# Gate and up products by seven block products instead of eight, with four feed-forward groups

## The chip, the cores and the metric

The kernel runs on one core of a Trainium2 chip. The metric is the device time of one execution in microseconds (us). Four engines matter here: TensorE (PE, with its weight loads shown as PEld), VectorE (DVE), ScalarE (ACT) and SyncE (SP), which only issues transfers. Each engine takes its instructions in the order in which the program lists them.

## The reference

One step of a two-layer network on 640 tokens (128 context tokens and 512 latent ones), in float32. Each layer is a feed-forward block, a mixer (an SSD scan with pooling in layer 0, a gated MLP with a convolution in layer 1) and a second feed-forward block. All three are modulated by vectors that come from `c` and `w_mod`. What the change touches is the feed-forward block, computed four times:

```python
def swiglu(h, w_gate, w_up, w_down):
    return (jax.nn.silu(h @ w_gate) * (h @ w_up)) @ w_down
# h (640, 1024), w_gate and w_up (1024, 2816), w_down (2816, 1024)
# x = x + 0.5 * gate * swiglu(modulate(rms_norm(x, g), shift, scale), ...)
```

## The kernel before

Activations lie transposed: eight tiles of 128 channels by 640 tokens hold the residual `x`. The tokens are worked on in two halves of 320, called A and B. Every float32 product is made of three TensorE products: each operand is split into a high part (a cast) and a low part (a subtraction), and `mm3` (L311 to L313) adds high by high, high by low and low by high into one PSUM bank. So a weight tile of 128 input rows by 128 output columns takes three matmuls of 320 columns for each half.

A feed-forward block (`ffn`) has 22 slices j of 128 hidden channels. For each slice, `run_units` makes gate and up for half A and then for half B, over eight input tiles k: 2 halves x 2 matrices x 8 x 3 = 96 matmuls. `post` then takes silu of gate on ScalarE (L551), multiplies by up on VectorE (L552) and splits the result with `split` (cast L296 on ScalarE, subtraction L297 on VectorE). The slices come in groups, `GROUPS`. After each group `out_phase` multiplies the group's slices by `w_down` for eight output tiles m and two halves, and `x_update` (L341) adds to `x`. The last group's out phase runs into `boundary`, which makes the next stage's modulated input: VectorE L303 and L307, ScalarE L305, first for half A and, while TensorE already works on A's first four weight units, for half B. The first four units are then used for half B too.

TensorE's order is the order of the program. VectorE, ScalarE and SyncE are ordered by Tile's scheduler before the run: an instruction whose inputs and buffers are there goes, and of several the one that is earlier in the program.

A weight unit is 128 x 1024 floats (512 KB). `load_raw` (L182) transfers it into a raw buffer, `load_unit` casts (L202) and subtracts (L203). A raw buffer is free again after its split. `W(key)` starts the loads of a unit and of the two after it in `plan`. The split tiles of gate and up units take two of the nine buffers of tag "w" each, and are free when TensorE has used them.

The modulation vectors are made on VectorE, next to all this: an item (`mod_item`) is a transfer of 512 KB (L247) into a buffer of the same raw tag and two multiply-and-reduce instructions (L250). There are 128 items. `pump(n)` emits the next n; `need_mod` emits until a given vector is done. In the first feed-forward block three are pumped per slice, later two, so all 128 are done within the third block. `odd`, the mixer of layer 1, begins with `boundary` and then `pump(1000)`, which finds none left; `even`, the mixer of layer 0, begins with `boundary` and `need_mod(0, 8)`, which finds that vector done.

## Time and profile before

| | us |
|---|---|
| median of 2 runs | 2660.35 (2659.68 to 2661.01) |
| span of the profiled execution | 2658.8 |
| TensorE busy | 2615.8 (98%) |
| VectorE busy | 1633.9 (61%) |
| ScalarE busy | 883.1 (33%) |
| transfers, mean over the span | 107 GB/s |

Read the busy shares first, then the chain of work that ended last, then busy time by stage. The stages follow each other at about 503 (first block ends, `even` begins), 853, 1315 (third block begins), 1784 (`odd` begins) and 2170 us. A busy time of TensorE counts pipelined matmuls that overlap, so the number of matmuls in a stretch says more than their durations.

### The profile page before, as it was taken

Reading aid. Unit: us, or ns where it says so; the run is one execution under the profiler, and the core shown is the slowest. Engines: PE = TensorE matmul, PEld = TensorE weight load, DVE = VectorE, ACT = ScalarE, POOL = GpSimd, SP = SyncE. Lnnn points to the kernel's source line nnn. Section 1 sums busy time; section 2 is a strip of 40 time slices with the busy share of each in tenths; the row PEclk is TensorE's granted clock in tenths of the full one; section 3 lists DMA queues with packets and bytes.
Section 4 is the critical chain, followed back from the end, with each engine's and each line's share of the span. In section 5 each row is a group of like instructions: output and inputs, shape, how many; then the busy total and the mean of one; then the engine's idle time right before and its main releaser. Section 6 shows DMA issues by size and latency. Waiting matters only on the chain.

```text
span 2658.8 us, 43502 instructions
## 1 busy us (share of the span) xinstructions
PE 2615.8 (98%) x18141; PEld 2550.1 (96%) x18141; DVE 1633.9 (61%) x2961; ACT 883.1 (33%) x1630; POOL 5.2 (0%) x83
## 2 busy tenths in 40 slices
PE   7999999999999999999999999999999999999998
PEld 5999999999989999999999999999879999999998
DVE  6866667698997755556675554265984764323325
ACT  4322222468854321212432121242222543212222
POOL 0000000000000000000000000000000000000000
PEclk9999999999999999999999999999999999999999
DMA  6553445111223333434243342224441132212211
GB/s 247 194 158 124 156 138 178 60 56 57 72 68 104 131 123 117 130 118 139 76 141 122 112 135 95 68 92 121 117 113 56 64 104 65 88 63 72 78 62 68
DMA packets 88228, 284.72 MB, mean 107 GB/s; under 512 B 11744, under 2 KB 18400, under 8 KB 87520
## 3 DMA queue, kind: packets, MB, share of 16 engines
q1 hardware_dynamic: 85072, 276.39, 32.3%
q10 hardware_dynamic: 2960, 5.56, 0.7%
q8 instruction: 142, 2.33, 0.4%
q14 instruction: 54, 0.44, 0.1%
HBM read 267.31 MB, written 3.67 MB: 102 GB/s over the span
## 4 chain that ended last, share of the span: by engine, by line
PE 95%; DVE 3%; ACT 1%; DMA 1%; issue 0%; ACTq 0%; DVEq 0%
PE ps L311 29%; PE ps L312 29%; PE ps L313 29%; PE ps L1075 1%; PE ps L502 1%; PE ps L962 1%; PE ps L1138 1%; PE ps L1140 1%; PE ps L1139 1%; PE ps L902 0%; PE ps L929 0%; PE ps L431 0%; DVE slab L307 0%; DVE tmp L303 0%; DVE tmp L291 0%
## 5 line engine op out<-in xcount | busy, mean ns | idle before, releaser
L312 PE MATMUL ps<-slab,wh 128*128 128x320 f32 (+1 forms) x5376 | 1662.1, 309 | 0.7 <-DVE slab L297 0.4
L311 PE MATMUL ps<-slab,wh 128*128 128x320 f32 x5280 | 1639.6, 311 | 1.1 <-DVE slab L966 0.9
L313 PE MATMUL ps<-slab,wl 128*128 128x320 f32 x5280 | 1632.2, 309 | 0.0
L312 PEld LDWEIGHTS ps<-slab,wh 128*128 128x128 f32 (+1 forms) x5376 | 1008.9, 188 | 3.6 <-DVE slab L297 0.9
L311 PEld LDWEIGHTS ps<-slab,wh 128*128 128x128 f32 x5280 | 990.9, 188 | 9.6 <-issue 4.5
L313 PEld LDWEIGHTS ps<-slab,wl 128*128 128x128 f32 x5280 | 990.6, 188 | 0.5
L203 DVE TENSOR_TENSOR wl<-wr,wh 128x1024 fp32r<-128x1024 f32 (+3 forms) x401 | 429.6, 1082 | 296.9 <-ACT wh L202 141.4
L202 ACT CAST wh<-wr 128x1024 fp32r<-128x1024 f32 (+3 forms) x401 | 369.1, 935 | 548.4 <-DMA wr<-in_wg 162.7
L250 DVE CUSTOM_DVE_ANT_0 junk<-wm,crow,cv 128x1024 bf16<-128x1024 f32 x256 | 328.4, 1283 | 127.3 <-DMA wm<-in_wm 123.6
L341 DVE SCALAR_TENSOR_TENSOR slab<-ps,mod,slab 128x128 f32<-128x128 f32 (+2 forms) x384 | 156.2, 434 | 217.2 <-PE ps L313 216.8
L296 ACT CAST slab<-tmp 128x320 fp32r<-128x320 f32 x200 | 90.6, 459 | 431.2 <-DVE tmp L552 424.4
L552 DVE TENSOR_TENSOR tmp<-tmp,ps 128x320 f32<-128x320 f32 x176 | 84.8, 484 | 204.9 <-PE ps L313 203.0
L551 ACT ACTIVATE tmp<-ps 128x320 f32<-128x320 f32 x176 | 76.2, 436 | 342.9 <-PE ps L313 342.7
L297 DVE TENSOR_TENSOR slab<-tmp,slab 128x320 fp32r<-128x320 f32 x200 | 96.8, 490 | 65.9 <-ACT slab L296 65.6
L1082 DVE SCALAR_TENSOR_TENSOR cacc<-pad,cv,cacc 128x655 f32<-128x655 f32 x112 | 100.9, 901 | 4.2 <-ACT cacc L1078 0.7
L280 ACT ACTIVATE tmp<-slab 128x320 f32<-128x320 f32 x112 | 53.2, 475 | 145.3 <-DVE slab L341 133.3
L284 DVE TENSOR_TENSOR tmp<-tmp,tmp 128x320 f32<-128x320 f32 x98 | 47.9, 490 | 37.4 <-ACT tmp L280 37.4
L305 ACT ACTIVATE slab<-tmp,mod 128x128 fp32r<-128x128 f32 (+1 forms) x120 | 50.4, 468 | 45.1 <-DVE tmp L303 43.8
L307 DVE SCALAR_TENSOR_TENSOR slab<-tmp,mod,slab 128x128 fp32r<-128x128 f32 (+1 forms) x120 | 46.6, 432 | 0.7 <-ACT slab L305 0.7
L303 DVE SCALAR_TENSOR_TENSOR tmp<-slab,mod,tmp 128x128 f32<-128x128 f32 (+1 forms) x120 | 46.8, 435 | 0.1
L647 DVE SCALAR_TENSOR_TENSOR cacc<-pad,cv,cacc 128x642 f32<-128x642 f32 x48 | 42.3, 882 | 1.5 <-ACT cacc L641 1.1
L311 PE MATMUL ps<-ydh,wh 128*128 128x320 f32 x128 | 39.7, 310 | 0.0
(201 smaller groups left out, 1229.1 us busy)
## 6 DMA issues: line engine op xcount, KB each, us to landing
wm<-in_wm SPq DMA_DIRECT2D x128, 512.0 KB, 3.8
wr<-in_wg SPq DMA_DIRECT2D x88, 512.0 KB, 4.0
wr<-in_wu SPq DMA_DIRECT2D x88, 512.0 KB, 3.5
wr<-in_wd SPq DMA_DIRECT2D x64, 448.0 KB, 3.3
wr<-in_wd SPq DMA_DIRECT2D x32, 512.0 KB, 4.1
wr<-in_wei SPq DMA_DIRECT2D x24, 512.0 KB, 3.5
wr<-in_woi SPq DMA_DIRECT2D x24, 512.0 KB, 4.1
rep<-pad SPq DMA_DIRECT2D x128, 83.4 KB, 2.8
```

The costliest lines, as they stand in the source:

```text
L202: S.copy(hi, raw[:, k0:k1, :])
L203: V.tensor_sub(lo, raw[:, k0:k1, :], hi)
L250: V.tensor_tensor_reduce(out=junk, in0=w, in1=mst["crow"][cond], scale=1.0, scalar=cvc("b_mod", L * 72 + idx * KC + c), op0=ALU.mult, op1= ...
L296: S.copy(hi, src)
L297: V.tensor_sub(lo, src, hi)
L311: TE.matmul(ps, lhsT=wh, rhs=xh, start=start, stop=False)
L312: TE.matmul(ps, lhsT=wh, rhs=xl, start=False, stop=False)
L313: TE.matmul(ps, lhsT=wl, rhs=xh, start=False, stop=stop)
L341: V.scalar_tensor_tensor(out=x[m][:, a:b], in0=ps[:, a - o:b - o], scalar=mcol(L, gidx, m, cond), in1=x[m][:, a:b], op0=ALU.mult, op1=ALU.add)
L551: S.activation(out=sg, in_=pg[:, :TH], func=AF.Silu)
L552: V.tensor_mul(sg, sg, pu[:, :TH])
L1082: V.scalar_tensor_tensor(out=ac, in0=pad[:, i:i + 655], scalar=cvc("dw_w", i * 8 + j), in1=ac, op0=ALU.mult, op1=ALU.add)
```

## The change

Gate and up of one slice are seen as a product of 2 x 2 blocks: the input channels in two halves (k 0 to 3, k 4 to 7), the tokens in halves A and B, the columns in gate and up. The eight block products (k half x token half x matrix) become seven, P1 to P7, by the Strassen-Winograd scheme, for slices j >= 2 of every block. The sums of weight blocks (`load_sums`) and of input blocks (`full` and the lines after it) are made on chip and split again. Products accumulate in three PSUM banks per slice; ScalarE copies intermediate results out (`tap`), VectorE combines them. `product_order` interleaves two slices. A sum unit takes two raw buffers and six "w" buffers. `w_down` units now take "w" buffers as well, and raw buffers are three for the whole program. Modulation items are pumped one per slice in the first block only, and one per output tile m in every out phase but a block's last. The pool of the modulation tiles moves from the right side of memory to the left, under the stage's own pool. There are four groups instead of three. The other edits rename slabs as pairs or quads of the same data.

```diff
-GROUPS = ((0, 8), (8, 15), (15, 22))
+GROUPS = ((0, 6), (6, 12), (12, 17), (17, 22))
...
+                        if j < NSTD:
+                            add_unit(("g", L, f, j), ap["wg"][L, f, j], 8, 128)
+                            add_unit(("u", L, f, j), ap["wu"][L, f, j], 8, 128)
+                        else:
+                            add_unit(("s", L, f, j), (ap["wg"][L, f, j], ap["wu"][L, f, j]), 8, 128)
...
+            raw = wpool.tile([P, n, m], F32, tag="raw", name=nm("wr"), bufs=RB)
...
+        def load_sums(key):
+            src, n, m = units[key]
+            g, u = raw_tile(src[0], n, m), raw_tile(src[1], n, m)
+            ph = state["pool"]
+            x1 = w_split(g, 8, m, tag="w", bufs=WB)
+            s31 = ph.tile([P, 8, m], F32, tag="s31", name=nm("ws"), bufs=1)
+            s24 = ph.tile([P, 8, m], F32, tag="s24", name=nm("ws"), bufs=1)
+            V.tensor_add(s31[:, 4:8, :], u[:, 0:4, :], u[:, 4:8, :])
+            V.tensor_add(s31[:, 0:4, :], u[:, 0:4, :], g[:, 0:4, :])
+            x2 = w_split(s31, 8, m, tag="w", bufs=WB)
+            V.tensor_add(s24[:, 0:4, :], g[:, 0:4, :], s31[:, 4:8, :])
+            V.tensor_add(s24[:, 4:8, :], g[:, 4:8, :], s24[:, 0:4, :])
+            x3 = w_split(s24, 8, m, tag="w", bufs=WB)
+            x4 = w_split(u[:, 4:8, :], 4, m, tag="w2", bufs=4, pool=ph)
+
+            def half(x, i):
+                return x[0][4 * i:4 * i + 4], x[1][4 * i:4 * i + 4]
+            loaded[key] = dict(P1=half(x1, 0), P2=half(x1, 1), P7=half(x2, 0), P5=half(x2, 1),
+                               P6=half(x3, 0), P3=half(x3, 1), P4=x4)
...
         def W(key):
-            prefetch(index[key] + LOOK)
+            i, left = index[key], LOOK
+            prefetch(i)
+            while i + 1 < len(plan) and left > 0:
+                i += 1
+                left -= 2 if plan[i][0] == "s" else 1
+                if wpos[0] <= i and plan[i][0] == "s" and not state.get("sums"):
+                    break
+                prefetch(i)
             return loaded[key]
...
-            w = state["raw"].tile([P, D], F32, tag="raw", name=nm("wm"), bufs=state["rb"])
+            w = wpool.tile([P, D], F32, tag="raw", name=nm("wm"), bufs=RB)
...
-        def out_phase(keys, sh, sl, L, gidx, last, nxt=None, lag=3):
+        def out_phase(keys, sh, sl, L, gidx, last, nxt=None, lag=3, items_per=0):
             if not last:
                 for m in range(8):
                     for H in (A, B):
                         out_task(H, m, keys[m], sh, sl, L, gidx, False)
+                    pump(items_per)
                 return None
...
+        CHAIN = (("P1", "P6", "P7", "P4"), ("P5", "P3"), ("P2",))
+
+        def product_order(js):
+
+            at = {j: [0, 0, 0] for j in js}
+            since = {}
+            out = []
+            while any(at[j][c] < len(CHAIN[c]) for j in js for c in range(3)):
+                t = len(out)
+                live = [j for j in js if any(at[j][c] < len(CHAIN[c]) for c in range(3))][:2]
+                cand = [(j, c) for j in live for c in range(3) if at[j][c] < len(CHAIN[c])]
+                cand = [(j, c) for j, c in cand if c == 0 or at[j][0] > 0]
+                ready = [jc for jc in cand if t - since.get(jc, -9) >= 3]
+                j, c = ready[0] if ready else min(cand, key=lambda jc: since.get(jc, -9))
+                out.append((j, CHAIN[c][at[j][c]]))
+                since[j, c] = t
+                at[j][c] += 1
+            return out
...
+            f12, f22, f11 = full(0, B), full(1, B), full(0, A)
+            V.tensor_sub(f22, f22, f12)
+            V.tensor_sub(f12, f11, f12)
+            V.scalar_tensor_tensor(out=f11, in0=f22, scalar=-1.0, in1=f11, op0=ALU.mult, op1=ALU.subtract)
+            X = dict(P1=hn.t[0, A], P2=hn.t[1, A], P3=hn.t[1, B])
+            X["P5"] = t_split(f12, ph, "T", 6)
+            X["P6"] = t_split(f11, ph, "T", 6)
+            X["P7"] = t_split(f22, ph, "T", 6)
+            f21 = full(1, A)
+            V.scalar_tensor_tensor(out=f21, in0=f11, scalar=-1.0, in1=f21, op0=ALU.mult, op1=ALU.subtract)
+            X["P4"] = t_split(f21, spool, "s", None)
...
+                for j, p in product_order(js):
+                    if p == "P1":
+                        W(("s", L, f, j))
+                    wh, wl = loaded["s", L, f, j][p]
+                    xh, xl = X[p]
+                    b = "a" if p in CHAIN[0] else "c" if p in CHAIN[1] else "b"
+                    if (j, b) not in bank:
+                        bank[j, b] = psum()
+                    ps = bank[j, b]
+                    first = p in ("P1", "P5", "P2")
+                    final = p in ("P4", "P3", "P2")
+                    for k in range(4):
+                        for n, (l, r) in enumerate(((wh, xh), (wh, xl), (wl, xh))):
+                            TE.matmul(ps[:, :TH], lhsT=l[k], rhs=r[:, k, :], start=(first and k == 0 and n == 0),
+                                      stop=(k == 3 and n == 2), skip_group_check=True)
+                    with tc.high_priority(offset=TAP_EARLY):
+                        if p in ("P1", "P6", "P7", "P5"):
+                            got[j, p] = tap(ps)
+                        if p == "P2":
+                            V.tensor_add(got[j, "P1"], ps[:, :TH], got[j, "P1"])
+                            S.activation(out=got[j, "P1"], in_=got[j, "P1"], func=AF.Silu)
+                        if p == "P3":
+                            V.tensor_add(got[j, "P6"], ps[:, :TH], got[j, "P6"])
+                            S.activation(out=got[j, "P6"], in_=got[j, "P6"], func=AF.Silu)
+                        if (p == "P7" and (j, "P5") in got) or (p == "P5" and (j, "P7") in got):
+                            V.tensor_add(got[j, "P7"], got[j, "P7"], got[j, "P5"])
+                        if p == "P4":
+                            hf = ph.tile([P, T], F32, tag="hf", name=nm("hf"), bufs=1)
+                            V.scalar_tensor_tensor(out=hf[:, SL[A]], in0=ps[:, :TH], scalar=-1.0, in1=got[j, "P1"],
+                                                   op0=ALU.mult, op1=ALU.mult)
+                            V.scalar_tensor_tensor(out=hf[:, SL[B]], in0=got[j, "P7"], scalar=-1.0,
+                                                   in1=got[j, "P6"], op0=ALU.mult, op1=ALU.mult)
+                            h_tile(j)
+                            split(hf, hts[j][:, 0, :], hts[j][:, 1, :])
+                    if p == "P1" and (L, f) == (0, 0):
+                        pump(1)
...
             for gi, (j0, j1) in enumerate(GROUPS):
-                for j in range(max(j0, 2), j1):
-                    for H in (A, B):
-                        pg, pu = run_units(H, keys[j], hnh, hnl)
-                        post(H, j, pg, pu)
-                    pump(3 if (L, f) == (0, 0) else 2)
+                products(range(max(j0, NSTD), j1))
+                if gi == len(GROUPS) - 1:
+                    state["sums"] = False
                 if gi < len(GROUPS) - 1:
                     need_mod(L, ig)
-                    out_phase([("d", L, f, gi, m) for m in range(8)], [hh[j] for j in range(j0, j1)],
-                              [hl[j] for j in range(j0, j1)], L, ig, False)
+                    out_phase([("d", L, f, gi, m) for m in range(8)], [hts[j][:, 0, :] for j in range(j0, j1)],
+                              [hts[j][:, 1, :] for j in range(j0, j1)], L, ig, False, items_per=1)
```

## Rows read from the trace of the kernel before

**Rows 1.** the page: busy time by engine, and the chain that ended last

```profile
PE 2615.8 (98%) x18141; PEld 2550.1 (96%) x18141; DVE 1633.9 (61%) x2961; ACT 883.1 (33%) x1630; POOL 5.2 (0%) x83
PE 95%; DVE 3%; ACT 1%; DMA 1%; issue 0%; ACTq 0%; DVEq 0%
```

**Rows 2.** windows by stage: PE, PEld, DVE, ACT, POOL busy (instructions), clock, DMA

```profile
853.00:1315.00 462.00, 462.00 (x3149) 461.68 (x3149) 272.20 (x469) 125.62 (x203) 0.00 (x0) 1.00 0.38 124
...
503.00:853.00 350.00, 339.13 (x2522) 324.97 (x2521) 304.76 (x693) 231.64 (x555) 2.47 (x41) 0.99 0.21 64
```

**Rows 3.** windows of 50 us, same columns, inside the second block

```profile
1000.00:1050.00 50.00, 50.00 (x343) 50.00 (x342) 25.56 (x49) 7.60 (x12) 0.00 (x0) 1.00 0.31 103
```

**Rows 4.** groups by line and shape, VectorE: count | busy us, mean ns | idle before

```profile
L250 DVE CUSTOM_DVE_ANT_0 junk<-wm,crow,cv 128x1024 bf16<-128x1024 f32 x256 | 328.4, 1283 | 127.3 <-DMA wm<-in_wm 123.6
L203 DVE TENSOR_TENSOR wl<-wr,wh 128x1024 fp32r<-128x1024 f32 x264 | 322.0, 1223 | 238.6 <-PE ps L312 133.4 <-ACT wh L202 91.6 <-issue 13.0
...
L297 DVE TENSOR_TENSOR slab<-tmp,slab 128x320 fp32r<-128x320 f32 x200 | 96.8, 490 | 65.9 <-ACT slab L296 65.6
...
L943 DVE TENSOR_TENSOR slab<-slab,slab 128x512 f32<-128x512 f32 x32 | 20.8, 685 | 4.7 <-ACT slab L937 4.7
...
L307 DVE SCALAR_TENSOR_TENSOR slab<-tmp,mod,slab 128x320 fp32r<-128x320 f32 x40 | 19.8, 547 | 0.7 <-ACT slab L305 0.7
...
L951 DVE TENSOR_TENSOR slab<-slab,slab 128x640 f32<-128x640 f32 x16 | 13.1, 820 | 0.8 <-ACT slab L941 0.7
```

**Rows 5.** groups by line and shape, ScalarE

```profile
L202 ACT CAST wh<-wr 128x1024 fp32r<-128x1024 f32 x264 | 275.4, 1048 | 429.9 <-DMA wr<-in_wg 162.7 <-PE ps L313 70.0 <-DMA wr<-in_wu 60.0
...
L296 ACT CAST slab<-slab 128x640 fp32r<-128x640 f32 x8 | 5.6, 725 | 4.0 <-PE ps L312 4.0
```

**Rows 6.** timeline of VectorE at the third block's start: start us, us, line [idle <-releaser]

```profile
1337.55 1.01 DVE L307 SCALAR_TENSOR_TENSOR slab<-tmp,mod,slab 128x320 fp32r<-128x320 f32 x2
...
1347.33 2.46 DVE L203 TENSOR_TENSOR wl<-wr,wh 128x1024 fp32r<-128x1024 f32 x2 [8.37 <-PE ps L312]
```

**Rows 7.** timeline of VectorE inside the first block

```profile
426.37 1.28 DVE L250 CUSTOM_DVE_ANT_0 junk<-wm,crow,cv 128x1024 bf16<-128x1024 f32 x1 [0.85 <-DMA wm<-in_wm]
...
428.91 1.22 DVE L203 TENSOR_TENSOR wl<-wr,wh 128x1024 fp32r<-128x1024 f32 x1
430.04 0.48 DVE L552 TENSOR_TENSOR tmp<-tmp,ps 128x320 f32<-128x320 f32 x1
...
430.51 1.28 DVE L250 CUSTOM_DVE_ANT_0 junk<-wm,crow,cv 128x1024 bf16<-128x1024 f32 x1
...
431.72 0.49 DVE L297 TENSOR_TENSOR slab<-tmp,slab 128x320 fp32r<-128x320 f32 x1
```

**Rows 8.** timeline of SyncE's issues, first group's out phase

```profile
130.36 2.99 SPq L182 DMA_DIRECT2D wr<-in_wd  x2
136.08 3.89 SPq L247 DMA_DIRECT2D wm<-in_wm  x3
142.48 20.52 SPq L182 DMA_DIRECT2D wr<-in_wd  x6
```

**Rows 9.** timeline of VectorE at the start of odd

```profile
1803.13 1.01 DVE L307 SCALAR_TENSOR_TENSOR slab<-tmp,mod,slab 128x320 fp32r<-128x320 f32 x2 [0.52 <-ACT slab L305]
1813.05 2.46 DVE L203 TENSOR_TENSOR wl<-wr,wh 128x1024 fp32r<-128x1024 f32 x2 [8.91 <-PE ps L312]
```

**Rows 10.** windows of 10 us at the start of even

```profile
530.00:540.00 10.00, 9.46 (x65) 9.43 (x66) 9.24 (x21) 5.06 (x10) 0.00 (x0) 1.00 0.00 0
540.00:550.00 10.00, 10.00 (x72) 9.99 (x71) 10.00 (x19) 3.30 (x8) 0.16 (x3) 1.00 0.09 29
```

**Rows 11.** windows with a lower clock, after TensorE had waited

```profile
30.00:35.00 5.00, 5.00 (x26) 1.92 (x26) 4.80 (x10) 1.60 (x4) 0.00 (x0) 0.66 1.00 423
...
580.00:590.00 10.00, 9.97 (x59) 9.84 (x60) 9.35 (x26) 7.45 (x21) 0.00 (x0) 0.83 0.01 2
...
760.00:770.00 10.00, 5.88 (x21) 4.37 (x21) 8.47 (x19) 8.05 (x19) 0.00 (x0) 0.83 0.27 80
```

More of the change, by code (lines that the diff above doesn't have):

```diff
@@ L90, in nm, with slab, pair, quad @@
             return f"{p}_{uid[0]}"
-        def slab(dt=F32, where="s", cols=T):
-            pool = spool if where == "s" else state["pool"]
-            return pool.tile([P, cols], dt, tag="s", name=nm("slab"))
+        def slab(dt=F32, cols=T):
+            return state["pool"].tile([P, cols], dt, tag="s", name=nm("slab"))
+        def pair():
+            return spool.tile([P, 2, T], F32R, tag="s", name=nm("pair"))
+        def quad():
+            return spool.tile([P, 4, TH], F32R, tag="s", name=nm("quad"))
+        class Rows:
+            def __init__(self):
+                self.t = [pair() for _ in range(KC)]
+            def hi(self, c, H):
+                return self.t[c][:, 0, SL[H]]
+            def lo(self, c, H):
+                return self.t[c][:, 1, SL[H]]
+        class Quads:
+            def __init__(self):
+                self.t = {}
+                for kh in range(2):
+                    for H in (0, 1):
+                        self.t[kh, H] = (quad(), quad())
+            def hi(self, c, H):
+                return self.t[c // 4, H][0][:, c % 4, :]
+            def lo(self, c, H):
+                return self.t[c // 4, H][1][:, c % 4, :]
         yclose = []
-        def open_phase(bufs, rb):
+        def open_phase(bufs):
             state["ctx"] = ExitStack()
             state["pool"] = state["ctx"].enter_context(tc.tile_pool(name=nm("phase"), bufs=bufs, reuse_waits="tile"))
-            state["raw"] = state["pool"]
-            state["rb"] = rb
         def close_phase():
@@ new lines, in w_split @@
+        def w_split(src, n, m, **kw):
+            pool = kw.pop("pool", wpool)
+            hi = pool.tile([P, n, m], F32R, name=nm("wh"), **kw)
+            lo = pool.tile([P, n, m], F32R, name=nm("wl"), **kw)
+            S.copy(hi, src)
+            V.tensor_sub(lo, src, hi)
+            return [hi[:, i, :] for i in range(n)], [lo[:, i, :] for i in range(n)]
+        def load_sums(key):
[16 more added lines that the diff above has]
+                               P6=half(x3, 0), P3=half(x3, 1), P4=x4)
@@ L197, in load_unit @@
-            his, los = [], []
-            for k0 in range(0, n, step):
-                k1 = min(n, k0 + step)
-                hi = pool.tile([P, k1 - k0, m], F32R, name=nm("wh"), **kw)
-                lo = pool.tile([P, k1 - k0, m], F32R, name=nm("wl"), **kw)
-                S.copy(hi, raw[:, k0:k1, :])
-                V.tensor_sub(lo, raw[:, k0:k1, :], hi)
-                his += [hi[:, i, :] for i in range(k1 - k0)]
-                los += [lo[:, i, :] for i in range(k1 - k0)]
-            loaded[key] = (his, los)
+            loaded[key] = w_split(raw, n, m, tag="w", bufs=WB)
@@ new lines, in ffn, with full, t_split @@
+            ph = state["pool"]
+            def full(kh, H):
+                t = ph.tile([P, 4, TH], F32, tag="h", name=nm("full"), bufs=6)
+                V.tensor_add(t, hn.t[kh, H][0], hn.t[kh, H][1])
+                return t
+            def t_split(src, pool, tag, bufs):
+                kw = dict(tag=tag, bufs=bufs) if bufs else dict(tag=tag)
+                hi = pool.tile([P, 4, TH], F32R, name=nm("th"), **kw)
+                lo = pool.tile([P, 4, TH], F32R, name=nm("tl"), **kw)
+                split(src, hi, lo)
+                return hi, lo
@@ new lines, in ffn, with tap, products @@
+            X["P4"] = t_split(f21, spool, "s", None)
+            def tap(src):
+                t = ph.tile([P, TH], F32, tag="tap", name=nm("tap"), bufs=6)
+                S.copy(t, src[:, :TH])
+                return t
+            def products(js):
+                bank, got = {}, {}
+                for j, p in product_order(js):
[30 more added lines that the diff above has]
+                                                   in1=got[j, "P6"], op0=ALU.mult, op1=ALU.mult)
+                            h_tile(j)
+                            split(hf, hts[j][:, 0, :], hts[j][:, 1, :])
+                    if p == "P1" and (L, f) == (0, 0):
+                        pump(1)
```

185 lines of the change are left out of this document (88 added, 97 removed).

## The prediction

> **What bounds the kernel now.** I read the page's busy shares first: TensorE is busy 98% of a span of 2658.8 us, VectorE 61%, and the chain that ended last is TensorE for 95% [rows 1]. The windows by stage then show where TensorE is never idle: the second feed-forward block runs 462.0 of 462 us, with VectorE at 272.2 [rows 2]. Inside it 50 us hold 343 matmuls, 145.8 ns from one to the next, and VectorE is busy for 25.56 of them [rows 3]. So in a feed-forward block time is the number of matmuls times 145.8 ns, until another engine cannot follow. The mixer `even` is different: VectorE is busy 304.8 of 350 us there and TensorE 339.1 [rows 2]; work added on VectorE in that stretch has little free time to go into.
>
> **What goes.** A slice j >= 2 takes 7 products x 4 k x 3 = 84 matmuls instead of 96, of the same shape. 20 slices in 4 blocks save 12 each: 960 matmuls, 960 x 145.8 ns = **-140.0 us** [rows 3]. Down products keep their number.
>
> **VectorE per slice.** Ends of neighbours overlap by 0.08 us, so I take durations less that. A sum unit: four additions of 512 (0.685), three subtractions of 1024 (1.223), one of 512: 2.4 + 3.4 + 0.6 = 6.5 us [rows 4]. After the products: three additions of 320 (0.490), two three-operand instructions of 320 (0.547), one subtraction of 640 (0.820): 1.2 + 0.9 + 0.7 = 2.9 us [rows 4]. Together 9.4 us, against 84 x 0.1458 = 12.2 us of TensorE: the cover holds, at 77%. In the first block an item comes on top: its pair of L250 takes 2.54 us from 426.37 to 428.91, about 2.65 with the small instruction that follows [rows 7], so 12.0 of 12.2. In the out phases an item per m joins a weight split and three updates, about 4.6 us against 4.4 (five slices) or 5.2 (six). ScalarE has three casts of 1024 (1.048), one of 512, four copies, two silu and a cast of 640 (0.725) [rows 5], near 7 us of 12.2: not a bound. For queueing where VectorE is full (first block, ends of out phases) I take **+8**, between 0 (12.0 still fits under 12.2) and 40 (2 us for each of the first block's 20 slices).
>
> **Start of each block.** TensorE meets its first sum unit when the first four units are through half B. In the third block that is at 1347.33, when buffers come free, and VectorE has just been idle for 8.37 us [rows 6]. Now it must make the input sums: four `full` additions, two subtractions and two three-operand instructions of 1280, then four subtractions for the splits. By the slope from 640 to 1024 (0.403 us for 384) [rows 4] a 1280 takes 1.41 us net, the twelve 17.1. They can begin once half B's modulated input is there, 1338.5 [rows 6], and all stand earlier in the program than the first sum unit's splits. At 1347.4 some 9.0 us are left, less the last subtraction (1.4), which waits for its cast, plus the posts of half B (1.6) and the low part of x1 (1.1): P1 starts about 10 us late, and P5, whose weights need two additions, a cast and a subtraction more, waits another 3. Three blocks x 13; in the first block the same work meets a shorter cover but an emptier VectorE, and I take 10: **+49**, between 12 (x1 slips into a gap; P5's wait alone) and 60.
>
> **Ends of groups.** The last slice ends P2, P7, P4. P4 adds into the bank that `tap` reads after P7, so TensorE waits for a 320 copy, about 0.7 us. Then P4's result goes through two 0.47, a cast 0.725 and a subtraction 0.82 [rows 4, 5]: 2.5 us and hand-overs of 0.1 to 0.2 each, while the out phase reaches the last slice's low part after 16 or 13 matmuls, 2.3 or 1.9 us. Floor: 1.4 us for each of 16 ends = 22. In-order queues add to it: at 430.51 an item started while the cast for a split was under way, and the subtraction that follows the multiply of 430.04 went only at 431.72 [rows 7]: 0.7 us later than the multiply (0.48) and a cast (0.46) take. With VectorE at 77% or more I take 0.6 us per end: **+32**, between 22 and 55. (The kernel before has 7 or 8 slices per group and a 320 tail: covered.)
>
> **Items that are left.** One per slice in the first block (20), 4 by `need_mod`, 8 in each of three out phases: 48 of the 56 of layer 0 by `even`, so `need_mod(0, 8)` now emits 8 there. The second and third block make 24 each, to 104; `pump(1000)` in `odd` emits **24**. Where they stand decides. SyncE issues transfers in program order, also past the point where weights are wanted: two `wd`, three `wm`, six `wd` [rows 8], just as the code lists them; and now items and weights share three raw buffers. In `odd` the units of the second slice pair (j = 2) are ahead of the 24, those of j = 3 behind. VectorE is full until 1804, one raw buffer is free until TensorE releases tiles at 1813.05 [rows 9], so two items pass by then. The other 22 take 22 x 2.65 = 58 us, other VectorE work 4 to 5: j = 3 has its weights at about 1876. TensorE has j = 2 alone, 96 x 0.1458 = 14 us, to 1827. It stands **+49**, between 35 (items start earlier) and 66 (next paragraph). In `even` two or three of the 8 fit before 530; five, 13 us, go into a VectorE that is 92% and 100% busy there [rows 10]: **+12**, between 3 and 25.
>
> **Memory.** The modulation pool now lies under the stage's own pool, so the mixer's first tiles can lie where the items still read. If the pads of j = 0 and 1 in `odd` are such tiles, TensorE does not even do j = 2 in the meantime: +14 there; in `even` up to +11. I take nothing of it in the sum; it is a rival.
>
> **The clock.** After TensorE had waited, its granted clock was 0.66 over 5 us and twice 0.83 over 10 us [rows 11]: each time 1.7 us of TensorE's time lost to the lower of its two levels, 1.2 GHz. Four new waits of 10 us and more (three starts, `odd`): **+7**, between 0 and 20. The Trainium skill, "TensorE: Matmul & The Clock Gate", section "HAM oscillation", says that gaps in matmul work put the clock back to the lower level and that this is paid anew after each gap; by it all 20 new waits count if long enough, 34 us instead of 7. Waits under 2 us at the group ends have no such row here, so I stay with four.
>
> **Sum.** -140 + 8 + 49 + 32 + 49 + 12 + 7 = +17 on the profiled execution's 2658.8 = 2676. The median of the runs is 1.5 above that span: **2677 us**.
>
> **Rivals.** (a) *Items hidden*: they pass before the mixers, or VectorE does them in gaps. For it: VectorE is idle 8.91 us before 1813.05 [rows 9]. Against it: the order of rows 8. 2677 - 49 - 12 - 2 = 2614. (b) *The feed-forward covers hold*: starts at 12, ends at 22, no queueing, three clock losses fewer: 2677 - 37 - 10 - 8 - 5 = 2617. For it: VectorE has 23% left and the scheduler fills gaps. Both: 2554. (c) *Weight tiles come late*, the other side: nine "w" buffers hold one and a half sum units, so the next unit's x2 can only be completed when P2 of this one is done, three products (5.2 us) before P5 wants it, x3 four (7.0 us) after P3. A subtraction of 1.2, or a cast and a subtraction of 2.3, have to get through VectorE's and ScalarE's queues in that time; it decides when queueing is over 4 us. At 1 us lost per slice, 80 slices: 2757. For it: the queue at 77 to 98% with single instructions of 1.2 us; against it: the slack is three such instructions. (d) *Memory overlap*: 2677 + 25 = 2702.
>
> **Chances.** My sum 0.35, and for itself between 2635 and 2715; (a) 0.15, (b) 0.18, both 0.08, (c) 0.16, (d) 0.08. For all, 2575 to 2750 leaves out the most of both (a) and (b), and the upper part of (c). About 2% (53 us: 2607 and 2713) is what a measurement of this kernel can tell from no change. Faster: both, half of (a), some of (b) and the sum's low end, 0.26. Slower: (c), some of (d) and the sum's high end, 0.23. Same 0.51.
>
> **What would show it.** Matmuls 960 fewer, 343 per 50 us in the middle of a group (fewer: (c)). TensorE idle about 50 us near the start of `odd`, ended by a weight split of j = 3 behind a run of L250's line (none: (a)). Gaps of 10 us and then 3 at the block starts, ended by VectorE's low part of x1 (none: (b)); 2 us at each group end, ended by the subtraction of `split`. Wrong at the root would be a matmul interval other than 145.8 ns, or a VectorE that is the chain for most of the span.

## The result and the profile after

| | before | after |
|---|---|---|
| median of the runs, us | 2660.35 | 2731.61 (2730.23 to 2732.99) |
| span of the profiled execution | 2658.8 | 2728.4 |
| TensorE busy | 2615.8 (98%) | 2519.4 (92%) |
| VectorE busy | 1633.9 (61%) | 2148.5 (79%) |
| ScalarE busy | 883.1 (33%) | 1163.0 (43%) |

The ratio of after to before is 1.0267, with a 95% interval of 1.0238 to 1.0297. The change makes the kernel slower, by 71 us; I had forecast 2677, which is 17 us slower and within what I called the same.

The page of the changed kernel answers [rows 1]: busy time by engine, and the chain that ended last.

```profile
PE 2519.4 (92%) x17181; PEld 2431.2 (89%) x17181; DVE 2148.5 (79%) x3737; ACT 1163.0 (43%) x2040; POOL 5.1 (0%) x83
PE 83%; DVE 12%; ACT 2%; DMA 1%; issue 1%; SPq 0%; DVEq 0%; ACTq 0%
```

TensorE has exactly 960 matmuls fewer (18141 before) and is busy 96 us less, but VectorE now holds 12% of the chain where it held 3%. The windows by stage answer [rows 2, 3] (PE, PEld, DVE, ACT, POOL busy with instructions, clock, DMA): the second block, `even`, `odd`, and 50 us inside a group.

```profile
881.00:1345.00 464.00, 441.08 (x2944) 436.14 (x2942) 367.84 (x611) 200.24 (x319) 0.00 (x0) 0.98 0.33 106
...
501.00:881.00 380.00, 341.16 (x2500) 324.66 (x2501) 322.19 (x717) 228.02 (x540) 2.25 (x38) 0.96 0.23 73
...
1804.00:2260.00 456.00, 399.18 (x2820) 358.28 (x2821) 339.39 (x551) 133.27 (x220) 1.37 (x24) 0.94 0.35 109
...
1000.00:1050.00 50.00, 50.00 (x343) 50.00 (x342) 40.98 (x70) 18.43 (x29) 0.00 (x0) 1.00 0.37 127
```

Inside a group nothing is lost: 343 matmuls in 50 us as before, with VectorE at 82%. But the second block has 23 us without TensorE where it had none, `even` 39 where it had 11, and `odd` 57 where it had less than one. The waits of TensorE say where (what was waited for: us in total, times, longest). L690 is the line of the products, L361 to L363 are the three matmuls of an ordinary unit or a down unit, L219 makes the low part of weights, L672 is `tap`, L354 and L356 write the modulated input at a block's end:

```profile
PE ps L361 <- ACT wh L218: 45.3, 1, 45.3
PE ps L690 <- DVE wl L219: 35.0, 5, 10.9
PE ps L868 <- ACT dtr L862: 23.7, 2, 20.8
...
PE ps L363 <- DVE wl L219: 16.1, 25, 1.5
PE ps L690 <- ACT tap L672: 8.5, 16, 0.6
PE ps L690 <- ACT th L345: 7.5, 1, 7.5
PE ps L361 <- ACT pair L354: 6.8, 2, 3.6
PE ps L362 <- DVE h L346: 6.5, 14, 0.8
PE ps L361 <- ACT quad L354: 5.9, 2, 4.3
PE ps L337 <- DVE tmp L333: 4.0, 3, 2.0
PE ps L1213 <- DMA rep<-pad: 3.2, 1, 3.2
PE ps L362 <- DVE pair L356: 2.5, 3, 1.2
```

**The low parts of late weights.** Of the 25 waits on L363, 24 come in fours: 4 x 0.48 us in the last out phase of each block, 4 x 0.87 us late in `even` and 4 x 0.88 late in `odd`. The kernel before has none of them. VectorE's side of the one at 1315.00:

```profile
1314.12 0.82 DVE L219 TENSOR_TENSOR wl<-wr,wh 128x640 fp32r<-128x640 f32 x1 [0.34 <-PE ps L362]
```

VectorE is not busy with something else there. It stood idle, and the subtraction waited for a matmul of TensorE, which frees a tile. Since the change `w_down` and the mixers' output weights take their tiles from the nine of tag "w". That this sharing is the cause is read from the trace and the code; no run gives the tiles back.

**The wait in `odd`** is the one forecast. Its rows in the timeline (start us, us, engine, line, in brackets the idle time before and who ended it):

```profile
1804.55 85.75 SPq L296 DMA_DIRECT2D wm<-in_wm  x24
1892.70 0.33 SPq L208 DMA_DIRECT2D wr<-in_woi  x1
...
1895.84 1.04 ACT L218 CAST wh<-wr 128x1024 fp32r<-128x1024 f32 x1 [43.71 <-DMA wr<-in_woi]
...
1892.78 1.28 DVE L299 CUSTOM_DVE_ANT_0 junk<-wm,crow,cv 128x1024 bf16<-128x1024 f32 x1
...
1896.94 0.64 PE L361 MATMUL ps<-pair,wh 128*128 128x320 f32 x1 [45.28 <-ACT wh L218]
```

SyncE spends 86 us on the 24 item transfers, one buffer at a time as VectorE frees it. The next weights are issued at 1892.70, ScalarE, idle for 43.71 us, casts them, and TensorE starts again.

**`even`** has the same picture with eight items, and something behind it:

```profile
501.54 38.33 SPq L296 DMA_DIRECT2D wm<-in_wm  x8
...
545.53 1.04 ACT L218 CAST wh<-wr 128x1024 fp32r<-128x1024 f32 x1 [20.33 <-DMA wr<-in_wei]
...
547.99 0.41 ACT L862 COPY dtr<-ps 32x320 f32<-32x320 f32 x1 [1.41 <-DVE mod L307]
...
548.46 0.42 PE L868 MATMUL ps<-cst,dtr 32*128 32x32 f32 x2 [20.83 <-ACT dtr L862]
```

The copy into `dtr` waits for L307, the last item's instruction, to which it has no relation in what is computed: the stage's tile lies where the item still reads. That is rival (d). Of the eight items one is done when TensorE stops at 527.6 (its L307 stands at 525.84); the other seven, 19 us of VectorE, run while TensorE stands.

**A block's start and end**, here the third's. The end's wait was in no term of mine:

```profile
1343.58 1.16 DVE L219 TENSOR_TENSOR wl<-wr,wh 128x1024 fp32r<-128x1024 f32 x1
...
1346.22 0.51 PE L361 MATMUL ps<-quad,wh 128*128 128x320 f32 x1 [4.29 <-ACT quad L354]
...
1369.93 4.29 DVE L648 TENSOR_TENSOR full<-quad,quad 128x1280 f32<-128x1280 f32 x3
...
1381.35 4.30 DVE L346 TENSOR_TENSOR tl<-full,th 128x1280 fp32r<-128x1280 f32 x3
1385.57 1.48 DVE L667 SCALAR_TENSOR_TENSOR full<-full,full 128x1280 f32<-128x1280 f32 x1
1386.97 1.22 DVE L219 TENSOR_TENSOR wl<-wr,wh 128x1024 fp32r<-128x1024 f32 x1
...
1388.24 0.64 PE L690 MATMUL ps<-quad,wl 128*128 128x320 f32 x1 [10.86 <-DVE wl L219]
```

Just ahead of the third block's modulated input (L352 at 1344.66) VectorE still splits one of its first weight units (L219). Later the input sums run on VectorE without a gap, the low part of the first sum unit's weights stands behind them, and TensorE has waited 10.86 us.

**The clock.** Windows of 2 us (PE busy, clock, DMA), first behind that wait, then behind the end of a group in the first block, where TensorE had waited 0.52, 1.56 and 0.77 us within 7 us:

```profile
1388.00:1390.00 2.00, 1.76 (x6) 0.50 0.36 113
1390.00:1392.00 2.00, 2.00 (x9) 0.50 0.38 150
1392.00:1394.00 2.00, 2.00 (x9) 0.50 0.00 0
...
362.00:364.00 2.00, 1.23 (x6) 0.84 0.47 115
364.00:366.00 2.00, 2.00 (x10) 0.50 0.13 49
366.00:368.00 2.00, 2.00 (x13) 0.81 0.59 193
```

At 0.50, which is the lower level of 1.2 GHz, one matmul begins 0.267 us after another (1390 to 1394 us), at the full clock 0.147. Busy time times what the clock lacks to 1, summed over all windows of 2 us, is 5.0 us in three stretches before and 28.9 us in thirteen stretches after. By the two intervals, which differ by less than a factor of 2, both sums are about a tenth too high.

Stage by stage (a stage begins with VectorE's first instruction of `apply_mod`; e1 to e9 are the experiments below):

| us | first block | even | second | third | odd | fourth and end |
|---|---|---|---|---|---|---|
| before | 503.3 | 347.2 | 467.1 | 465.6 | 393.4 | 482.2 |
| after | 501.4 | 379.3 | 463.9 | 459.8 | 455.7 | 468.2 |
| e1 items one per slice | 499.9 | 379.7 | 470.2 | 462.8 | 401.9 | 468.2 |
| e2 pool at the other end | 505.8 | 373.2 | 459.8 | 458.7 | 451.5 | 467.9 |
| e3 three ordinary slices | 500.0 | 379.1 | 458.1 | 457.8 | 457.8 | 465.9 |
| e4 last group of six | 499.5 | 378.8 | 462.8 | 457.5 | 455.5 | 468.4 |
| e5 third slice after sums | 500.8 | 379.4 | 450.8 | 451.3 | 457.3 | 458.4 |
| e6 no items at the mixers | 503.9 | 354.8 | 467.6 | 464.5 | 402.3 | 468.5 |
| e7 together | 497.4 | 357.1 | 462.1 | 452.1 | 402.7 | 458.6 |
| e8 before, four groups | 504.4 | 344.1 | 468.6 | 467.2 | 393.3 | 482.5 |
| e9 sums on GpSimd | 543.6 | 355.3 | 503.2 | 480.7 | 402.4 | 463.2 |

Each block has 240 matmuls or 35 us less to do; the four gained 2, 3, 6 and 14.

### The profile page after: what moved, and what is told of

It is laid out like the page before. It is cut to its first block, busy times and chain, and to the rows that moved or that the text cites. A ratio compares the mean times of both kernels' runs of the same rounds, so it can differ in the third digit from the quotient of the medians.

```text
span 2728.4 us, 43038 instructions
## 1 busy us (share of the span) xinstructions
PE 2519.4 (92%) x17181; PEld 2431.2 (89%) x17181; DVE 2148.5 (79%) x3737; ACT 1163.0 (43%) x2040; POOL 5.1 (0%) x83
## 4 chain that ended last, share of the span: by engine, by line
PE 83%; DVE 12%; ACT 2%; DMA 1%; issue 1%; SPq 0%; DVEq 0%; ACTq 0%
PE ps L690 35%; PE ps L362 14%; PE ps L363 14%; PE ps L361 14%; DVE junk L299 3%; DVE wl L219 2%; PE ps L1213 1%; PE ps L550 1%; DVE tmp L352 1%; PE ps L1277 1%; PE ps L1279 1%; PE ps L1278 1%; PE ps L1100 1%; DVE h L346 1%; DVE tl L346 1%
## 5 line engine op out<-in xcount | busy, mean ns | idle before, releaser
L218 ACT CAST wh<-wr 128x1024 fp32r<-128x1024 f32 (+3 forms) x393 | 338.7, 864 | 611.6 <-PE ps L363 216.3
L219 DVE TENSOR_TENSOR wl<-wr,wh 128x1024 fp32r<-128x1024 f32 (+3 forms) x393 | 388.6, 990 | 155.8 <-issue 58.4
L363 PE MATMUL ps<-h,wl 128*128 128x320 f32 x1408 | 437.4, 311 | 7.6 <-DVE wl L219 7.6
L362 PE MATMUL ps<-h,wh 128*128 128x320 f32 x1408 | 437.4, 311 | 6.5 <-DVE h L346 6.5
L361 PE MATMUL ps<-h,wh 128*128 128x320 f32 x1408 | 436.7, 310 | 1.6 <-ACT h L345 1.6
L690 PE MATMUL ps<-quad,wh 128*128 128x320 f32 x1920 | 428.5, 311 | 0.0
L690 PE MATMUL ps<-th,wh 128*128 128x320 f32 x1280 | 399.7, 312 | 16.0 <-ACT tap L672 8.5
L690 PE MATMUL ps<-th,wl 128*128 128x320 f32 x1280 | 397.7, 311 | 2.6 <-DVE wl L219 2.6
L690 PE MATMUL ps<-tl,wh 128*128 128x320 f32 x1280 | 397.7, 311 | 1.5 <-DVE tl L346 1.5
L361 PE MATMUL ps<-pair,wh 128*128 128x320 f32 (+1 forms) x976 | 310.7, 318 | 54.8 <-ACT wh L218 45.3
L690 PE MATMUL ps<-quad,wl 128*128 128x320 f32 x960 | 299.5, 312 | 32.3 <-DVE wl L219 32.3
L690 PEld LDWEIGHTS ps<-quad,wh 128*128 128x128 f32 x1920 | 324.3, 190 | 0.0
L362 PE MATMUL ps<-pair,wh 128*128 128x320 f32 (+1 forms) x976 | 305.7, 313 | 2.5 <-DVE pair L356 2.5
L363 PE MATMUL ps<-pair,wl 128*128 128x320 f32 (+1 forms) x976 | 305.3, 313 | 1.5 <-DVE wl L219 1.5
L363 PEld LDWEIGHTS ps<-h,wl 128*128 128x128 f32 x1408 | 264.9, 188 | 11.8 <-DVE wl L219 11.8
L362 PEld LDWEIGHTS ps<-h,wh 128*128 128x128 f32 x1408 | 264.8, 188 | 10.7 <-DVE h L346 10.1
L361 PEld LDWEIGHTS ps<-h,wh 128*128 128x128 f32 x1408 | 264.9, 188 | 2.1 <-ACT h L345 1.8
L690 PEld LDWEIGHTS ps<-th,wh 128*128 128x128 f32 x1280 | 242.3, 189 | 20.7 <-ACT tap L672 12.7
L219 DVE TENSOR_TENSOR wl<-ws,wh 128x1024 fp32r<-128x1024 f32 x160 | 194.1, 1221 | 79.0 <-PE ps L690 70.9
L690 PEld LDWEIGHTS ps<-th,wl 128*128 128x128 f32 x1280 | 242.1, 189 | 3.2 <-DVE wl L219 3.1
```

Source lines behind the costliest of these rows:

```text
L218: S.copy(hi, src)
L219: V.tensor_sub(lo, src, hi)
L361: TE.matmul(ps, lhsT=wh, rhs=xh, start=start, stop=False)
L362: TE.matmul(ps, lhsT=wh, rhs=xl, start=False, stop=False)
L363: TE.matmul(ps, lhsT=wl, rhs=xh, start=False, stop=stop)
L690: TE.matmul(ps[:, :TH], lhsT=l[k], rhs=r[:, k, :], start=(first and k == 0 and n == 0), stop=(k == 3 and n == 2), skip_group_check=True)
```

## The experiments

**e1: the items of `odd` done beside the slices.**

```diff
-                    if p == "P1" and (L, f) == (0, 0):
+                    if p == "P1":
                         pump(1)
```

> The items of the modulation are issued one per slice in all four blocks instead of the first alone, so that none is left when the mixer odd begins (56 by the end of the first block's neighbourhood, 44 more in the second block, the last 28 in the third). Theory: TensorE's 45.3 us wait on L218 in odd is the 24 items queued ahead of the weights of j = 3, in the transfers' order and on VectorE. Then odd shortens by the wait and by some 5 us of low clock after it, from 455.7 to about 405 us, and the time is about 2681 us (2672 to 2692). Rival: an item beside a slice overfills VectorE (12.0 of 12.2 us), and the second and third block become longer by 20 us or more: 2700 us or more. Second rival: the wait in odd has another cause (the stage's own tiles); it stays, and the time with it: 2725 to 2740.

Measured: 2686.66 us (2684.51 to 2688.35), 1.0096 times before (1.0083 to 1.0110), 45 us less than after. `odd` as a stage:

```profile
1813.00:2215.00 402.00, 396.21 (x2825) 357.02 (x2826) 276.41 (x439) 132.90 (x221) 0.58 (x9) 0.99 0.30 91
```

TensorE is busy 396 of 402 us, and the 45.3 us wait on L218 is no longer among its waits. The 24 items were its cause. `odd` gained 53.8 us, but the second and third block lost 6.3 and 3.0. That is the rival in part: the waits for `tap` at the ends of groups grew from 8.5 to 14.2 us.

**e2: the modulation pool at the other end of the memory.**

```diff
-            mst["pool"] = mst["ctx"].enter_context(tc.tile_pool(name=nm("modw"), bufs=1,
+            mst["pool"] = mst["ctx"].enter_context(tc.tile_pool(name=nm("modw"), bufs=1, side="right",
```

> One argument is added: the modulation pool is laid at the other end of the memory again, as in the kernel before; nothing else changes. Theory (memory overlap): TensorE's 20.8 us wait in even on the copy of dtr (L862), which itself waits for the last item's instruction (L307), is there because dtr and the transfers of its weights lie where the items still read. Without the overlap it goes, with some 3 us of low clock: even falls from 379 to about 357 us, the time to about 2708 us (2700 to 2716). Rival: VectorE's eight items hold even back wherever they lie (21 us of VectorE work); then the wait only changes its name and the time stays at 2725 to 2735.

Measured: 2722.04 us (2718.69 to 2722.33), 9.6 less than after; `even` 373.2, 6.1 less. Neither theory: the wait for `dtr` is gone, but these have come among TensorE's waits, or grown (L1015, 1.6 in after):

```profile
PE ps L925 <- ACT slab L795: 7.8, 1, 7.8
...
PE ps L1015 <- ACT slab L795: 4.7, 1, 4.7
...
PE ps L903 <- DVE nfb L909: 1.8, 1, 1.8
```

The mixer starts earlier (`dtr` is copied at 531 instead of 548), meets VectorE with the same items in its queue and waits for its convolutions instead. The overlap is real, but it set the place of the wait more than its length. (The other stages moved by -4 to +4 us in this run; I have no reason for those.)

**e6: no items at either mixer.** On top of e1, the line that emits the last eight items at the head of `even` is deleted. They hold the second block's gate, and the `need_mod` of its first group asks for them there.

```diff
             hn, pa = boundary(first, 0, 4, 3, prev, Rows)
-            need_mod(0, 8)
             close_mod()
```

> Items one per slice in all blocks, and the line at the head of even that emits the last eight items of layer 0 is deleted (they are the second block's gate, wanted at the end of its first group); so no item stands at either mixer. Theory: the eight items cost even their 21 us of VectorE work and the low clock behind it, wherever they lie: even falls from 380 to about 350 us, and eight more items beside slices cost 2 us: 2686.7 - 28 = about 2659 us (2652 to 2666). Rival: even is longer for other reasons (weights late since items and weights share three raw buffers, the stage's memory); then it stays over 365 us and the time over 2672.

Measured: 2664.83 us (2660.66 to 2669.15), 1.0016 times before (1.0007 to 1.0025); `even` 354.8, 24.9 less than in e1. Eight items are 8 x 2.65 = 21 us of VectorE, and that with the clock behind it is about what they cost. Of the 32 us that `even` had lost, 25 are the eight items'; the four waits on L363 are still there (3.5 us).

**e3: three ordinary slices per block.**

```diff
-NSTD = 2
+NSTD = 3
...
             state["sums"] = True
             ph = state["pool"]
+            for j in range(2, NSTD):
+                for H in (A, B):
+                    pg, pu = run_units(H, keys[j], hn)
+                    post(H, j, pg, pu)
```

> Three slices per block are computed with eight products instead of two, 48 matmuls or 7 us more in all; the third slice's 96 matmuls (14 us) now stand between half B and the first sum unit. Theory: TensorE waits about 10.5 us at each block's start because VectorE has some 20 us of input sums and splits to make; with 14 us more of cover these waits go, with 1 to 2 us of low clock after each. Gain 4 x (10.5 + 1.5) - 7 = 41: about 2691 us (2683 to 2703). Rival: the wait belongs to the first sum unit's weights (raw buffers, tiles), and stands after the third slice just as long: 2735 to 2742.

Measured: 2720.64 us (2718.43 to 2721.68), 11 less than after and in neither range. The waits became shorter, not none: 3.59 and 2.23, together 5.8 us, instead of 10.9 in the third block (the 6.9 in the next expectation is too much). Its timeline:

```profile
1367.85 2.46 DVE L219 TENSOR_TENSOR wl<-wr,wh 128x1024 fp32r<-128x1024 f32 x2 [7.26 <-PE ps L362]
...
1388.71 0.41 PE L694 MATMUL ps<-th,wh 128*128 128x320 f32 x1 [3.59 <-ACT th L345]
1391.35 0.64 PE L694 MATMUL ps<-tl,wh 128*128 128x320 f32 x1 [2.23 <-DVE tl L346]
```

VectorE stood 7.26 us before the third slice's weights, which wait for tiles that TensorE frees, while the input sums, with everything they need there, were behind it in the queue. Order, not only amount.

**e5: the third slice issued behind the input sums.** The loop of e3 stands ahead of the loop over the groups instead.

> Three slices per block with eight products, as in the run before, but the third slice is issued behind the input sums. There VectorE had stood idle for 7.26 us (until 1367.85) on the ordinary third slice's weights, which waited for tiles that TensorE releases, with the input sums behind them in its queue; TensorE then waited 6.9 us for th and tl. Theory: the start costs what VectorE's queue has in it between half B's input and P5's operands, and an order without that idle stretch takes the 6.9 us away with 1 us of low clock: 3 x 8 in the second to fourth block and up to 8 in the first, from 2720.6 to about 2692 us (2686 to 2702). Rival: the amount of VectorE's work alone sets the start; then the order is no matter: 2716 to 2724.

Measured: 2700.79 us (2699.01 to 2701.92), 1.0152 times before (1.0137 to 1.0168), 20 less than e3. The second, third and fourth block gained 7.3, 6.5 and 7.5 us over e3, a little less than the 8 forecast; the first gained nothing, so the time is 9 over my figure, though inside the range. No wait at the first sum unit of these three blocks is over 1.5 us, and the low clock of the second block is gone (5.3 us in after, 0.0 here), although this kernel has 48 matmuls more.

**e4: the last group with six slices.**

```diff
-GROUPS = ((0, 6), (6, 12), (12, 17), (17, 22))
+GROUPS = ((0, 6), (6, 11), (11, 16), (16, 22))
```

> The groups have 6, 5, 5 and 6 slices instead of 6, 6, 5 and 5. Theory: with five slices in a block's last group only 45 matmuls (6.6 us) follow the last half A output, and TensorE waits 3 to 4 us for the first modulated input at a block's end (3.15, 4.29 and 3.60 us before L361). With six, 54 matmuls (7.9 us) follow: each wait is 1.3 us shorter, and the clock falls less; 5 to 10 us in all: 2721 to 2727 us. Rival: the wait is set by VectorE's and ScalarE's own queue at the block's end, not by the number of matmuls: no difference, 2730 to 2734.

Measured: 2724.95 us (2722.48 to 2727.61), 6.7 less than after. Of the waits at the blocks' ends the 3.15, 4.29 and 3.60 us became 2.3 each. As the theory said, the matmuls that follow the last half A output are cover, and this change had cut them from 63 (seven slices) to 45. Whether 45 are too few by themselves, the next run tells.

**e8: four groups alone, on the kernel before.**

```diff
-GROUPS = ((0, 8), (8, 15), (15, 22))
+GROUPS = ((0, 6), (6, 12), (12, 17), (17, 22))
```

> The kernel before, with four groups of 6, 6, 5 and 5 slices instead of 8, 7 and 7, and nothing else changed. Theory: a group's end costs TensorE time only because the last of seven products ends in a chain of 2.5 us; with ordinary slices, whose last post is a 320-wide tail, four ends are covered as three were, and the 16 additional updates per block fit into VectorE's 61%: 2658 to 2666 us. Rival: the number of groups costs by itself (shorter down sums, updates of x, a shorter tail at the block's end): 2675 us or more, and then some of what was put down to the products belongs to the groups.

Measured: 2662.47 us (2661.75 to 2667.24), 1.0009 times before (1.0000 to 1.0018). TensorE is busy as before, 98%:

```profile
PE 2615.4 (98%) x18141; PEld 2549.1 (96%) x18141; DVE 1673.8 (63%) x3089; ACT 889.9 (33%) x1662; POOL 5.4 (0%) x83
```

The groups by themselves cost 2 us. What a group's end costs in the changed kernel belongs to the products and to a VectorE that is already at work. The same holds for a block's end. Here, too, only 45 matmuls follow the last half A output, and the wait for the first modulated input (ScalarE's line is L305 in this kernel) is

```profile
PE ps L311 <- ACT slab L305: 1.9, 3, 0.7
```

0.7 us at most, against 3.15 to 4.29 in after. So the shorter cover alone costs little. In this run the first weights of the third block are all split by 1300.3, 17 us before VectorE begins the modulated input of half A (1317.1); in after the splits run until 1344.7, right up to it.

**e7: four edits together.** Those of e6, e5 and e4.

> Four edits together: items one per slice and none at the mixers, three ordinary slices per block with the third behind the input sums, and groups of 6, 5, 5 and 6. Theory: the losses are separate places of TensorE's time and add up: 2659 - 29 (block starts) - 11 (the third slice alone) - 6 (block ends) = about 2613 us (2600 to 2628), below the kernel before. Rival: VectorE is full (items beside every slice, an ordinary slice's work on top), and what one edit gives back another takes: 2635 or more.

Measured: 2629.39 us (2628.44 to 2632.10), 0.9885 times before (0.9872 to 0.9899). It beats both kernels, by 31 and 102 us. It is 16 us over my forecast and just outside the range, but not far over its parts as they were measured: e6's 2664.8, less the 30.8 us of e5 and the 6.7 of e4, is 2627. My forecast had been made from the forecasts of the parts, e6 6 us too low and e5 9. So the losses are separate places and, over the whole, nearly add up. Only the second block falls short. Two of its stretches:

```profile
1000.00:1050.00 50.00, 48.88 (x334) 48.62 (x333) 47.51 (x76) 26.86 (x44) 0.00 (x0) 1.00 0.38 126
...
1200.00:1250.00 50.00, 50.00 (x343) 50.00 (x342) 49.71 (x80) 27.41 (x45) 0.00 (x0) 1.00 0.40 132
```

In the first TensorE has waited once, 1.12 us for a low part (L219), and does 334 matmuls; in the second VectorE is busier still, 49.71 us with an item beside each slice, and TensorE does all 343. So a full VectorE need not slow the products. By its parts this block would have 467.6 - 13.1 - 1.1 = 453.4 us, and it has 462.1. Against e5 its waits behind the start are 14.1 us instead of 6.7, most of them around the ends of groups, and the clock takes 4.6 us where e5 had no drop. About half of what is lost here comes back in the first (-4) and third block (-2); the others differ by up to 3 us.

**e9: the weight additions on GpSimd.** On top of e7, to take 2.4 us per slice off VectorE (the 16 us of its expectation are those over my forecast, before I had set e7 against its measured parts):

```diff
-            V.tensor_add(s31[:, 4:8, :], u[:, 0:4, :], u[:, 4:8, :])
+            G.tensor_add(s31[:, 4:8, :], u[:, 0:4, :], u[:, 4:8, :])
```

and so for the other three.

> The four edits together as in the run before, and the four weight additions of each sum unit (lines 229 to 233, 2.4 us of VectorE's time per slice, 76 slices, 183 us in all) are put on GpSimd, which has been idle. Theory: what the four edits together gave back (16 us, most of it in the second block, where 50 us held 334 matmuls and VectorE was busy for 47.51 of them) is VectorE being full with an item beside every slice; with 183 us less on it the second block falls from 462 to about 451 us, the first by some 5, and the time to 2605 to 2618 us. Rival: the addition takes so much longer on GpSimd, or slows VectorE's instructions beside it, that the chain from the additions over the cast and the subtraction to P5's and P6's weights comes late in every slice: then over 2640 us.

Measured: 2750.08 us (2745.59 to 2758.35), 1.0341 times before (1.0323 to 1.0359). The rival, for both of its reasons. GpSimd's costliest group and TensorE's largest sum of waits:

```profile
L232 POOL TENSOR_TENSOR ws<-wr,ws 128x512 f32<-128x512 f32 x76 | 147.3, 1938 | 47.9 <-DVE wl L219 32.5 <-ACT tap L672 15.4
```

```profile
PE ps L690 <- ACT tap L672: 101.2, 75, 7.1
```

An addition of 512 takes 1.7 to 1.9 us there, 0.685 on VectorE [rows 4]. And in the timeline:

```profile
1033.29 1.30 POOL L229 TENSOR_TENSOR ws<-wr 128x512 f32<-128x512 f32 x1 [60.77 <-DMA wr<-in_wu]
...
1033.29 1.32 DVE L304 TENSOR_SCALAR mod<-mod,cv 128x2 f32<-128x2 f32 x1
...
1055.95 1.04 ACT L218 CAST wh<-ws 128x1024 fp32r<-128x1024 f32 x1 [2.04 <-POOL ws L233]
1056.90 0.42 ACT L672 COPY tap<-ps 128x320 f32<-128x320 f32 x1
...
1057.37 0.64 PE L690 MATMUL ps<-th,wh 128*128 128x320 f32 x1 [7.12 <-ACT tap L672]
```

`tap`, for which TensorE has waited 7.12 us, stands in ScalarE's queue behind a cast that waits for GpSimd's sum. And L304 on 128x2, which takes 0.22 us in e7, took 1.32 beside a GpSimd instruction of 1.30 that began at the same moment. The relief of VectorE was eaten: it is busy 2134.8 us, against 2113.6 in e7 with the additions on it. So this run doesn't show what VectorE's fullness costs e7, only that GpSimd is no way out of it. (The 334 matmuls of its expectation are those of the first stretch above; the second, with a fuller VectorE, speaks against that theory.)

## Why the prediction was right and wrong, step by step

The sum against the rows of after, all as after less before, in us of the profiled execution:

| term | forecast | measured | from |
|---|---|---|---|
| 960 matmuls | -140.0 | -140.0 | count, and 343 per 50 us again |
| VectorE queueing | 8 | 2.6 | L690 on L219 at 98 and 191 us, in the first block (of the 35.0) |
| late weights' low parts | none | 14.6 | L363 on L219, 24 of 25: 7.6 in out phases, 3.5 in `even`, 3.5 in `odd` |
| block starts | 49 | 41.4 | 32.4 of the 35.0 + 7.5 (L690 on L219 and `th`) + 1.5 on `tl`, not shown above |
| ends of groups | 32 | 16.6 | 8.5 (`tap`) + 6.5 and 1.6 (h; the second not shown above) |
| `odd` | 49 | 50.0 | 45.3 + 3.2 (rep) + 1.5 (L363, just behind them) |
| `even` | 12 | 21.7 | 23.7 less 2.0 before |
| block ends | none | 17.0 | 19.8 in L361 and L362 on L354, L356, and L337, less 2.8 before |
| clock | 7 | 23.9 | 28.9 less 5.0 |
| other waits | none | 2.1 | the rest of TensorE's idle time, 166.0 in all |
| not placed | none | 19.7 | what is left of the span's 69.6 |
| sum | +17 | +69.6 | |

**The mechanisms were there.** The cover in the middle of a group holds, with VectorE near the 77% that I had worked out (82% in the window shown); rival (c) did not occur: 343 matmuls per 50 us. The wait in `odd` was where I put it, for the reason I gave, and nearly of the size, 45.3 on 49; e1 took it away. (In the sum for the starts, twelve times 1.41 are 16.9 and not 17.1; nothing hangs on that.) The starts have the 10 us (10.7, 10.9, 10.7). The 3 us that I added for P5 did not come as a wait: in the third block the additions for P5's weights were done by 1370, before the input sums.

**Where it failed.** The sum is 53 us short. Five things make it:

*The block ends, 17.* The change part by part has no line for what a shorter last group does at the block's end. I counted down products as "keeping their number" and did not ask what their order covers. Seven slices cover the first modulated input with 63 matmuls or 9.2 us; five leave 45, or 6.6, and in after the waits of 3 to 4 us follow. e4 shows that more cover shortens them. But e8 has the same 45 and waits 0.7 us at most, so the larger part must come from what the changed kernel has there besides; in the third block a split of the next weights stands just ahead of the modulated input (1343.58 above). That this is the cause, and how the 17 us divide, no run shows.

*The late low parts, 15.* That `w_down` takes "w" tiles now stands in the change part by part, and I gave it no term. TensorE waits for low parts whose subtraction waits for TensorE to free a tile. The 7.6 us of the out phases come near the 8 of my term for VectorE's queue, but that would be luck: VectorE was idle in front of almost all of these subtractions. What the queue itself cost is 2.6.

*The clock, 17.* I took four drops of 1.7 us. There are ten more than before, at 2.4 us each: 1.7 is what the drops of [rows 11] had cost, but at the start of the third block the low clock took 3.0. And I left out the waits under 10 us. "Waits under 2 us at the group ends have no such row here" was a gap in the evidence that I read as zero, and not even a full one: the drop at 580 in [rows 11] stands behind a wait of 1.29 us. Of the ends of groups one was followed by a drop (that at 362), most were not; each of the three waits of 3 to 4 us at the ends of blocks was. The Trainium skill, "TensorE: Matmul & The Clock Gate", section "HAM oscillation", which says that the low level is paid again after each gap, would have given 34 us by my own reading in the prediction; this trace has 24, nearer to it than my 7, though not after every wait.

*`even`, 10, and its rival.* I let three of eight items pass in gaps and charged five, 13 us, at VectorE's time. The rows show seven, 19 us, in TensorE's way. I had priced rival (d) at up to 11 here, and the wait for `dtr` looks like just that. But e2 and e6 correct this reading: without the overlap 6 us come back, without the items 25. The mis-sized step is the number of items that fit into gaps; the overlap is the smaller part. In `odd` it did no harm: j = 2 went ahead as forecast.

*What is not placed, 20.* In TensorE's rows a matmul lasts 0.31 us while the next begins 0.15 later, so at each wait up to 0.16 us of standing still counts as busy. Counted from the starts of the 320-wide matmuls (L361 to L363 and L690), what the waits hide in this way is 12.7 us at 72 waits, and 0.4 us at two before. Another 6 us more than before lie in intervals that are longer than 0.147 us and yet have no wait in the list. What is left is small, about 1 us by this table and 3 with the tenth that the clock's sum is too high; it stays open.

**Against it** the ends of groups were over-priced: 1.0 us each where I said 2.0, and 1.4 as a floor. TensorE waited 0.52 to 0.57 us for `tap` where I took 0.7, and the low part of P4's result came no more than 0.8 us late. The tail of 2.5 us less its cover of 2.3 or 1.9 us is 0.2 or 0.6, so the hand-overs and the queue that I had put on top came to little. With the starts and the queue this took back 28 us, and hid part of what I had left out; without it the sum would have been 81 us short.

The forecast of "the same" thus rested on +17 and a range to 2750, which holds the result. The chance of slower, 0.23, was too low because four of the terms had their error on the same side: they all count the places where TensorE stops, and I had counted too few.

## What to carry to other kernels

A saving of 140 us in products is worth that only where TensorE is the chain, and each place where it stops can cost twice, once as a wait and once as a lower clock behind it: list the places (starts, ends of groups and of blocks, mixers) and ask of each which matmuls cover it after the change, in count and in order, and which tiles its operands share. Work that used to be hidden beside the removed instructions has to be found again: here 32 small items had lost their cover, and putting them back beside the slices (e6) was worth 67 us of the 71. And an engine that looks free may not be one: the additions moved to GpSimd cost 121 us and left VectorE as busy as it was.

## What the runs showed of the hardware

The clock can fall behind short waits, not only behind a long one: after 0.52, 1.56 and 0.77 us within 7 us it was 0.84, 0.50 and 0.81 in three windows of 2 us, which cost about 1.5 us. Behind the other 15 ends of groups, with about 1 us of waits each, no window shows a drop. At the lower level a matmul of 320 columns took 0.267 us from start to start, against 0.147, which is 1.8 times.

GpSimd and VectorE stand in each other's way: an instruction of 2 elements on VectorE took 1.32 us beside one of 1.30 us on GpSimd, 0.22 without; the mean of the items' instruction rose from 1276 in e7 to 1472 ns in e9, that of the 320-wide additions of L702 from 484 to 1018. The Trainium skill, "SBUF — State Buffer", section "SBUF: two separate sides", says that the two engines share a pair of ports, and that a GpSimd instruction and a VectorE instruction in a two-port mode or with two inputs in SBUF lock each other out of it for a whole instruction. The durations of 1.30 and 1.32 us agree with that; in which mode L304 ran, no run shows.
